# Experts' rows gathered before the layer norm's scale and bias, and memory's products ahead of the capacity test

## The chip, the core and the metric

The kernel runs on one core of a Trainium2 chip, as one program. The metric is the device time of one execution in microseconds. Of every version several executions are timed and the median is compared; one execution more is profiled. The engines are TensorE (PE; its weight loads are shown as PEld), VectorE (DVE), ScalarE (ACT), GpSimd (POOL) and SyncE (SP). Each has its own queue and works it off in order. SyncE issues nearly all loads of weights here.

## The reference

Everything is float32, on 256 tokens of 1024 channels. The first block has two layers (a mixer, a layer norm, a feed-forward part, a layer norm); in layer 1 the feed-forward part is a mixture of eight experts with two experts a token. The second block has an FFN, a second mixer that also attends to a memory of 256 tokens, and another FFN.

```python
for l in range(2):
    mix = hybrid_mixer(x, ...)
    x = layer_norm(ALPHA * x + mix, ln_mix_g[l], ln_mix_b[l])
    ff = swiglu(x, ...) if l % 2 == 0 else moe_swiglu(x, router, w1, w3, w2)
    x = layer_norm(ALPHA * x + ff, ln_ffn_g[l], ln_ffn_b[l])

def moe_swiglu(x, w_router, w1, w3, w2):
    logits = x @ w_router
    gates = softmax(top2(logits))
    # rows of x are sorted by expert; each expert e computes on its rows
    y = (silu(xb @ w1[e]) * (xb @ w3[e])) @ w2[e]
    # y times its gate is added back at the token's place

x = x + 0.5 * swiglu_ffn(rms_norm(x, ffn1_norm), ffn1_w_in, ffn1_w_out)
mem_kv = rms_norm(mem, mem_norm) @ w_mem_kv
m_k, m_v = split(mem_kv);  m_k = rms_norm(m_k per head, m_k_gain)
```

## The kernel before, in words

Products keep float32's precision by splitting: each operand is a high part (`wh`, `xTh`) and a low part (`wl`, `xTl`), and `mm3` makes three matmuls (lines 183 to 185). `part` (L172, L174) makes the parts of a weight tile of 128x1024: ScalarE copies the high part, VectorE subtracts for the low one. `load` (L166) puts SyncE's DMA of 1 MB (two such tiles) into the next of a list of buffers, `self.places`. In front of every FFN, SyncE runs ahead as far as buffers are free.

The expert stage is the function `moe`. Ahead of it, `layer_norm_T` normalises the rows (L852), transposes them (L857) and applies scale and bias by channel while it evicts the transposed tiles (L859, L860); L862 and L863 split them into `xT`. Then it applies scale and bias to the rows themselves from the tile `rows` (L867), since the experts' inputs are gathered from rows. `moe` computes the router's logits from `xT` (`lg`, L907), the two largest (L913 to L917), and each token's place in its expert (`t_pos`, L921 to L925). L930 and L931 split the rows into `xtokh` and `xtokl`.

`gather` (L980 to L1003) is a matmul of those with a one-hot matrix `oh`, 128 slots at a time, which gives the transposed inputs of one expert: `xeh` and `xel` for the four experts with most tokens ("full", 128 slots), `xef` for two pairs of the others (64 slots each). High and low rows are accumulated in two halves of a PSUM bank, which are evicted by ScalarE and VectorE (L996, L998, L1000). For each of 42 steps (expert or pair, by block of 512 hidden channels) `up` makes the products `a_up` and the gated `mos` (L1025, L1026), and `down` transposes `mos` (`t_hT`, L1032) and multiplies by the third weight (`y_y`). `combine` scales by the gate and adds the rows back by a matmul `t_comb` (L1068 to L1070) to the accumulator `acc`, which starts as x times ALPHA (L1113). Inputs of later experts are gathered between the steps.

After the last step, `memory_load` fetches memory's transposed rows (`memT`) and the weights of its keys and values (`mem_k`, `mem_v`). A test follows (L1157, L1159): `mxi` says how many rows found no place among an expert's slots; only then a loop computes them. For the data here it is skipped, but every engine loads the number and branches. After it come `layer_norm_x` (L872 on), `rms_T` (L1228 on: squares L1234, logarithm and exponential L293 and L294, scaling L1239, transposes L267, eviction L277 and L278), and `memory_keys`: 48 matmuls for the keys (`a_pA`), 48 for the values (`a_pB`), the normalisation per head (`norm_heads`, L1263 to L1267), and the copy of the values (L1346). Then the second block's first FFN starts, its first products being `a_pA<-xTh,wh` again.

The order in each queue is set by the tile framework's scheduler, which works through the program in dependence order by its own estimates; `issue_after` is a hint to it. So the order of a queue isn't that of the code. ScalarE's functions come in tables: `table` asks for a set by name (`LOGEXP` has Ln and Exp, `SILU` Silu), and the compiler adds a load (ACT_TABLE_LOAD) wherever a function isn't in the set at hand.

```python
    def part(self, raw, o=0, m=1024):
        wh = self.wp.tile([P, 1024], F32R, name="wh")
        nc.scalar.activation(wh[:, :m], raw[:, o:o + m], AF.Copy)
        wl = self.wp.tile([P, 1024], F32R, name="wl")
        nc.vector.tensor_tensor(wl[:, :m], raw[:, o:o + m], wh[:, :m].bitcast(F32), op=ALU.subtract)
```

Of the kernel before, what the change touches and what calls it, by code (L numbers as in the profile page):

```python
# [9 lines left out]
F32 = mybir.dt.float32  # L10
F32R = mybir.dt.float32r
BF16 = mybir.dt.bfloat16
I32 = mybir.dt.int32
# [15 lines left out]
NE = 8  # L29
# [74 lines left out]
class Net:  # L104
# [737 lines left out]
    def layer_norm_T(self, tp, tag, r, st, rows, name, n=4, z_="lnz", bufs=4):  # L842
# [58 lines left out]
    def moe(self, fp, x, xT):  # L901
# [23 lines left out]
        V.tensor_scalar(pos, pos, -1.0, None, op0=ALU.add)  # L925

# [50 lines left out]
        def gather(u, g):  # L977

            src = pos if u == (0,) else poss
            o = oh[u] = fp.tile([P, 2, P], F32R, name="oh", bufs=2)  # L980
            w = P // len(u)
            for t in range(2):
                for i, s in enumerate(u):
                    V.tensor_scalar(o[:, t, i * w:i * w + w], iota[:, :w], src[:, t, s:s + 1], None, op0=ALU.is_equal)
            if len(u) == 1:
                g += [fp.tile([P, 8, P], F32R, name=f"xe{c}", tag=f"xe{c}{u[0] % 2}") for c in "hl"]
            else:
                g += [fp.tile([P, 8, P], F32, name="xef")]
            for k in range(0, 8, 2):
                pg = self.ps("t", "gat").rearrange("p (a k n) -> p a k n", a=2, k=2)  # L990
                for j in range(2):
                    for a, src in enumerate((xh, xl)):
                        for t in range(2):
                            PE.matmul(pg[:, a, j, :], src[:, t, (k + j) * P:(k + j) * P + P], o[:, t],
                                      start=t + a + j == 0, stop=t == 1, skip_group_check=True)
                S.activation(g[0][:, k:k + 2, :], pg[:, 0], AF.Copy)  # L996
                if len(u) == 1:
                    self.last = V.tensor_copy(g[1][:, k:k + 2, :], pg[:, 1])  # L998
                else:
                    self.last = V.tensor_tensor(g[0][:, k:k + 2, :], g[0][:, k:k + 2, :], pg[:, 1], op=ALU.add)  # L1000
                if k == 6 and u != (0,):
                    back[u] = places(u)
                yield  # L1003
# [54 lines left out]
        def combine(py, ohT, gp):  # L1058
# [5 lines left out]
            for t in range(2):  # L1064
                for h in range(2):
                    hs = slice(h * 512, h * 512 + 512)
                    pc = self.ps("t", "comb")
                    PE.matmul(pc, ohT[:, t, :], yh[:, hs], start=True, stop=False)  # L1068
                    PE.matmul(pc, ohT[:, t, :], yl[:, hs], start=False, stop=True)
                    V.tensor_tensor(acc[:, t, hs], acc[:, t, hs], pc, op=ALU.add)  # L1070

# [40 lines left out]
        with self.tc.issue_after(self.last.ins):  # L1112
            V.tensor_scalar(acc, x, ALPHA, None, op0=ALU.mult)  # L1113
# [8 lines left out]
        for n, (u, b) in enumerate(order):  # L1122
            if n == 1:
                self.places = [(fp, f"early{i}") for i in range(EARLY)] + [(fp, "rows"), (self.ap, "xTh"), (self.ap, "xTl")] + self.places
            if n in begin:
# [15 lines left out]
        st = self.new_stats()  # L1141

        def stats():
            for t in range(2):
                for h in range(2):
                    V.bn_stats(out=st[:, t, h, :], in_=acc[:, t, h * 512:h * 512 + 512])


        cap, mxf, mxi = fp.tile([P, NE], F32, name="cap"), fp.tile([P, 1], F32, name="mxf"), fp.tile([P, 1], I32, name="mxi")
        V.tensor_scalar(cap, rank, 3.5, 64.0, op0=ALU.is_lt, op1=ALU.mult)  # L1150
        V.tensor_scalar(cap, cap, 64.0, None, op0=ALU.add)
        V.tensor_tensor(pos, pos, cap[:, None, :].to_broadcast([P, 2, NE]), op=ALU.subtract)
        V.tensor_tensor(cap, cnt, cap, op=ALU.subtract)
        V.tensor_reduce(mxf, cap, axis=AX.X, op=ALU.max)
        V.tensor_scalar(mxf, mxf, 0.0, None, op0=ALU.max)
        V.tensor_copy(mxi, mxf)
        most = nc.values_load(mxi[0:1, 0:1], min_val=0, max_val=T)  # L1157
        stats()
        with self.tc.If(most > 0):  # L1159
            ecur = fp.tile([P, 1], F32, name="ecur")  # L1160
            V.memset(ecur, 0.0)
            with self.tc.For_i(0, NE, 1) as e:
# [18 lines left out]
                for k in range(8):  # L1181
# [4 lines left out]
                    V.tensor_copy(x2[:, k, :], pg[:, :P])  # L1186
# [37 lines left out]
                stats()  # L1224
# [623 lines left out]
def build(tc, A, out):  # L1848
    with ExitStack() as ctx:
# [18 lines left out]
        with net.banks(a=2, y=4, t=2), pool("moe") as fp:  # L1868
            rows = net.load_rows(fp.tile([P, 2, D], F32, name="rows"), "ln_mix", 2, 2)
            xT = net.layer_norm_T(fp, "t", r, st, rows, "mix1", z_="mos", bufs=2)  # L1870
            r, st, mem = net.moe(fp, r, xT)
# [3 lines left out]
            net.memory_keys(fp, *mem)  # L1875
# [28 lines left out]
```

## Time and profile before

| | |
|---|---|
| median of 3 runs | 2171.85 us (2169.86 to 2173.09) |
| profiled execution's own time | 2181.34 us |
| its span in the profile | 2179.6 us |
| busy: TensorE, VectorE, ScalarE | 96%, 60%, 47% |
| mean granted clock of TensorE | 0.965 of full speed |
| DMA, mean over the span | 250 GB/s |
| the expert stage with its ends | about 605 to 1560 us of the span |

The profiled execution is 9.5 us longer than the median of the timed ones; positions in the trace belong to it. A row of the trace in order of time gives start, duration, engine, line, operation, output tile and input tiles with shapes, how many instructions were merged (x), and in brackets the engine's idle time just before with what ended it. Buffer numbers are left out of names. Suffix q (PEq, SPq) means an engine's sequencer: branches, waits, DMA issues.

### The profile page before, as it was taken

What the parts mean: (1) busy time and instruction counts of PE and PEld (TensorE: products, weight loads), DVE (VectorE), ACT (ScalarE), POOL (GpSimd) and SP (SyncE); (2) the same over time, 40 slices, a digit from 0 to 9 for tenths busy, and PEclk for the clock granted to TensorE, in tenths of its full rate; (3) what the DMA queues carried; (4) which work ended last, traced back from release to release, by engine and by line L of the source; (5) the groups of instructions that cost most, each with busy time, mean ns of one, the idle gap of its engine ahead of it and who ended that gap; (6) DMA issues with size and microseconds to landing.
All of it is one profiled execution on the core that took longest, in us unless ns stands there. A gap on an engine that the chain in (4) does not pass through costs nothing. (4 is left out here: it accounts for less than half of the span.)

```text
span 2179.6 us, 31865 instructions
## 1 busy us (share of the span) xinstructions
PE 2085.4 (96%) x12770; PEld 1606.4 (74%) x12770; DVE 1301.9 (60%) x1911; ACT 1021.4 (47%) x1453; POOL 13.0 (1%) x27
## 2 busy tenths in 40 slices
PE   8998999899979999999999999999799999999998
PEld 7887999788766565566565566554799988888997
DVE  6767954766676555555465455443655568665544
ACT  6545444464545444444354345442544444544443
POOL 0000000000000000000000000000000000000000
PEclk9979999998979999999999999999899999999999
DMA  6313675322359999999999999998455553444552
GB/s 236 103 44 117 213 261 179 136 88 98 140 181 348 363 407 381 412 419 376 404 367 396 387 404 406 417 415 352 171 188 191 187 176 125 136 164 155 184 183 97
DMA packets 78987, 545.37 MB, mean 250 GB/s; under 512 B 8960, under 2 KB 11272, under 8 KB 13936
## 3 DMA queue, kind: packets, MB, share of 16 engines
q1 hardware_dynamic: 76112, 527.40, 63.4%
q0 software_dynamic: 2720, 15.86, 2.0%
q8 instruction: 103, 1.69, 0.3%
q14 instruction: 52, 0.43, 0.1%
HBM read 536.74 MB, written 6.49 MB: 249 GB/s over the span
## 5 line engine op out<-in xcount | busy, mean ns | idle before, releaser
L174 DVE TENSOR_TENSOR wl<-raw,wh 128x1024 fp32r<-128x1024 f32 (+1 forms) x662 | 798.1, 1217 | 436.4 <-ACT wh L172 422.4
L172 ACT ACTIVATE wh<-raw 128x1024 fp32r<-128x1024 f32 (+1 forms) x662 | 690.6, 1054 | 629.0 <-PE a_pA L184 276.1
L183 PE MATMUL a_pA<-xTh,wh 128*128 128x256 f32 x1456 | 421.0, 290 | 5.9 <-ACT foxqk L620 3.3
L185 PE MATMUL a_pA<-xTh,wl 128*128 128x256 f32 x1456 | 417.9, 287 | 0.9 <-DVE wl L174 0.9
L184 PE MATMUL a_pA<-xTl,wh 128*128 128x256 f32 x1456 | 418.2, 287 | 0.0
L183 PEld LDWEIGHTS a_pA<-xTh,wh 128*128 128x128 f32 x1456 | 283.4, 195 | 13.7 <-ACT foxqk L620 5.3
L184 PEld LDWEIGHTS a_pA<-xTl,wh 128*128 128x128 f32 x1456 | 283.5, 195 | 4.8 <-issue 3.4
L185 PEld LDWEIGHTS a_pA<-xTh,wl 128*128 128x128 f32 x1456 | 283.3, 195 | 4.2 <-issue 2.7
L1021 PE MATMUL a_up<-raw,xef 128*64 128x512 f32 x896 | 213.5, 596 | 0.0
L184 PE MATMUL a_up<-wl,xeh 128*128 128x512 f32 x448 | 180.7, 403 | 0.5 <-DVE wl L174 0.4
L183 PE MATMUL a_up<-wh,xeh 128*128 128x512 f32 x448 | 177.3, 399 | 0.0
L185 PE MATMUL a_up<-wh,xel 128*128 128x512 f32 x448 | 177.1, 395 | 0.0
L1021 PEld LDWEIGHTS a_up<-raw,xef 128*64 128x64 f32 x896 | 65.2, 137 | 127.7 <-issue 122.6
L183 PE MATMUL a_pB<-wh,xTh 128*128 128x256 f32 x480 | 142.0, 297 | 5.0 <-ACT glu L620 3.1
L1026 DVE TENSOR_TENSOR mos<-mos,a_up 128x512 f32<-128x512 f32 x42 | 28.7, 684 | 192.2 <-PE a_up L1021 141.5
L184 PE MATMUL a_pB<-wl,xTh 128*128 128x256 f32 x480 | 140.4, 293 | 0.0
L185 PE MATMUL a_pB<-wh,xTl 128*128 128x256 f32 x480 | 139.4, 293 | 0.6 <-DVE xTl L278 0.6
L1054 PE MATMUL y_y<-raw,mof 128*64 128x512 f32 x448 | 132.8, 602 | 0.7 <-ACT mof L1040 0.7
L184 PEld LDWEIGHTS a_up<-wl,xeh 128*128 128x128 f32 x448 | 84.6, 189 | 35.1 <-issue 12.2
L183 PEld LDWEIGHTS a_up<-wh,xeh 128*128 128x128 f32 x448 | 84.6, 189 | 27.5 <-ACT wh L172 7.3
L185 PE MATMUL acc_acc<-wh,ffl 128*128 128x512 f32 x264 | 102.0, 392 | 0.0
L184 PE MATMUL acc_acc<-wl,ffh 128*128 128x512 f32 x264 | 101.9, 392 | 0.0
(558 smaller groups left out, 2717.9 us busy)
## 6 DMA issues: line engine op xcount, KB each, us to landing
raw<-in_moe_w_dram SPq DMA_DIRECT2D x336, 1024.0 KB, 9.3
raw<-in_ffn_in_dram SPq DMA_DIRECT2D x44, 1024.0 KB, 4.8
raw<-in_ffn_w_dram SPq DMA_DIRECT2D x33, 1024.0 KB, 4.9
raw<-in_w_in_a_dram SPq DMA_DIRECT2D x24, 1024.0 KB, 5.0
raw<-in_ffn_out_dram SPq DMA_DIRECT2D x22, 1024.0 KB, 4.8
raw<-in_w_out_dram SPq DMA_DIRECT2D x12, 1024.0 KB, 4.9
raw<-in_w_in_g_dram SPq DMA_DIRECT2D x12, 1024.0 KB, 4.9
raw<-in_w_in_b_dram SPq DMA_DIRECT2D x6, 1024.0 KB, 5.0
```

What stands on the lines that cost most here:

```text
L172: nc.scalar.activation(wh[:, :m], raw[:, o:o + m], AF.Copy)
L174: nc.vector.tensor_tensor(wl[:, :m], raw[:, o:o + m], wh[:, :m].bitcast(F32), op=ALU.subtract)
L183: mm(out, lh, rh, start=start, stop=False, skip_group_check=True)
L184: mm(out, lh, rl, start=False, stop=False, skip_group_check=True)
L185: mm(out, ll, rh, start=False, stop=stop, skip_group_check=True)
L1021: PE.matmul(ps[r], xe[0][:, k0, r], w[:, k * 512:k * 512 + 512], start=k0 == 0, stop=k0 == 7, skip_group_check=True)
L1026: V.tensor_tensor(s, s, pp[1], op=ALU.mult)
L1054: PE.matmul(py[h][r], hf[:, k, r], w[:, j * 1024 + h * 512:j * 1024 + h * 512 + 512], start=b == 0 and k == 0, stop=b == 6 and k == 3, ski ...
```

## The change

1. `layer_norm_T` gets `None` for `rows`, and the rows are left without scale and bias. They are split and gathered as they are; high and low rows add up in one PSUM region, and scale (`gain`) and bias (`shift`) are applied by channel when the gathered tile is evicted. For a full expert the result is split there.
2. The accumulator therefore starts from the normalised rows with scale, bias and ALPHA, in four instructions.
3. The count of missing places (`overflow`) is written ahead of step 4, the statistics of the last layer norm inside the last `combine`.
4. `memory_products` makes memory's 96 products and evicts both halves into `keptm` ahead of the test; `memory_keys` only normalises the keys, behind it. The buffers for `mem_k`, `mem_v` and `memT` change places.

```diff
-        with self.tc.issue_after(last.ins):
-            for t in range(2):
-                for i, op in enumerate((ALU.mult, ALU.add)):
-                    V.tensor_tensor(r[:, t, :], r[:, t, :], rows[:, i], op=op)
+        if rows is not None:
+            with self.tc.issue_after(last.ins):
+                for t in range(2):
+                    for i, op in enumerate((ALU.mult, ALU.add)):
+                        V.tensor_tensor(r[:, t, :], r[:, t, :], rows[:, i], op=op)
...
-                pg = self.ps("t", "gat").rearrange("p (a k n) -> p a k n", a=2, k=2)
+                pg = self.ps("t", "gat")[:, :T].rearrange("p (k n) -> p k n", k=2)
...
-                            PE.matmul(pg[:, a, j, :], src[:, t, (k + j) * P:(k + j) * P + P], o[:, t],
-                                      start=t + a + j == 0, stop=t == 1, skip_group_check=True)
-                S.activation(g[0][:, k:k + 2, :], pg[:, 0], AF.Copy)
+                            PE.matmul(pg[:, j, :], src[:, t, (k + j) * P:(k + j) * P + P], o[:, t],
+                                      start=t + a + j == 0, stop=a + t == 2, skip_group_check=True)
+                z = fp.tile([P, 2, P], F32, name="gz", bufs=2) if len(u) == 1 else g[0][:, k:k + 2, :]
+                for j in range(2):
+                    last = S.activation(z[:, j, :], pg[:, j, :], AF.Identity, scale=gain[:, k + j:k + j + 1], bias=shift[:, k + j:k + j + 1])
                 if len(u) == 1:
-                    self.last = V.tensor_copy(g[1][:, k:k + 2, :], pg[:, 1])
-                else:
-                    self.last = V.tensor_tensor(g[0][:, k:k + 2, :], g[0][:, k:k + 2, :], pg[:, 1], op=ALU.add)
+                    S.activation(g[0][:, k:k + 2, :], z, AF.Copy)
+                    self.last = V.tensor_tensor(g[1][:, k:k + 2, :], z, g[0][:, k:k + 2, :].bitcast(F32), op=ALU.subtract)
...
-            V.tensor_scalar(acc, x, ALPHA, None, op0=ALU.mult)
+            for t in range(2):
+                V.scalar_tensor_tensor(acc[:, t, :], x[:, t, :], ALPHA, rows[:, 0], op0=ALU.mult, op1=ALU.mult)
+                V.scalar_tensor_tensor(acc[:, t, :], rows[:, 1], ALPHA, acc[:, t, :], op0=ALU.mult, op1=ALU.add)
...
-        self.places = [(fp, "early2"), (fp, "early3")]
-        mem = self.memory_load(fp, ("early0", "early1"))
+        free = [i for i in self.places if i[1].startswith("early")]
+        self.places = free[:2]
+        mem = self.memory_load(fp, [i[1] for i in free[2:4]])
         self.places = [(self.raw, "raw")] * 4
-        combine(py[prev[0]], *back[prev[0]])
...
+        combine(py[prev[0]], *back[prev[0]], last=True)
+        mem = self.memory_products(fp, *mem)
+
+
         most = nc.values_load(mxi[0:1, 0:1], min_val=0, max_val=T)
-        stats()
         with self.tc.If(most > 0):
...
-    def memory_keys(self, fp, mT, raw, parts):
-
-        kept = self.keep_mem(fp, tag="y")
-        ps = self.proj_a(None, mT, parts=parts[:2])
+    def memory_products(self, fp, mT, raw, parts):
+
+        kept = self.keep_mem(fp, tag="xeh1")
+        self.nc.scalar.activation(self.mkT, self.proj_a(None, mT, parts=parts[:2]), AF.Copy)
+        self.nc.scalar.activation(self.mv, self.proj_b(None, mT, parts=[parts[2], self.part(raw[1], 1024)]), AF.Copy)
+        return kept
+
+    def memory_keys(self, fp, kept):
+
+        ps = self.mkT
         self.table(SILU, self.norm_heads(fp, ps, 2, self.col2("mkg"), self.mkT.rearrange("p c t -> p (c t)"), "y", "mos"))
-        ps = self.proj_b(None, mT, parts=[parts[2], self.part(raw[1], 1024)])
-        self.nc.scalar.activation(self.mv, ps, AF.Copy)
...
-            xT = net.layer_norm_T(fp, "t", r, st, rows, "mix1", z_="mos", bufs=2)
-            r, st, mem = net.moe(fp, r, xT)
+            xT = net.layer_norm_T(fp, "t", r, st, None, "mix1", z_="mos", bufs=2)
+            r, st, mem = net.moe(fp, r, xT, rows)
```

What the change moves in the queues is seen at three places. Line numbers of the changed kernel are a few higher (L930 became L934, L931 L935, L1032 L1037, L1234 L1249).

VectorE's queue at the layer norm and the router (`lnz` and `xTl` are tiles of `xT`, `lg` the logits), before:

```order
L860 TENSOR_SCALAR lnz<-t_tr,p_72 128x256 x2
L863 TENSOR_TENSOR xTl<-lnz,xTh 128x512 x2
L867 TENSOR_TENSOR x<-x,rows 128x1024 x3
L174 TENSOR_TENSOR wl<-raw,wh 128x1024
L867 TENSOR_TENSOR x<-x,rows 128x1024
L907 COPY lg<-t_pSt 128x16
L931 TENSOR_TENSOR xtokl<-x,xtokh 128x1024
L913 MAX m_6584<-lg 128x8 x2
L931 TENSOR_TENSOR xtokl<-x,xtokh 128x1024
L914 MAX_INDEX i_6587<-m_6584,lg 128x8 x2
```

and now:

```order
L935 TENSOR_TENSOR xtokl<-x,xtokh 128x1024
L860 TENSOR_SCALAR lnz<-t_tr,p_72 128x256
L935 TENSOR_TENSOR xtokl<-x,xtokh 128x1024
L860 TENSOR_SCALAR lnz<-t_tr,p_72 128x256
L863 TENSOR_TENSOR xTl<-lnz,xTh 128x512 x2
L860 TENSOR_SCALAR lnz<-t_tr,p_72 128x256 x2
L863 TENSOR_TENSOR xTl<-lnz,xTh 128x512 x2
L174 TENSOR_TENSOR wl<-raw,wh 128x1024
L909 COPY lg<-t_pSt 128x16
L915 MAX m_6580<-lg 128x8 x2
L916 MAX_INDEX i_6583<-m_6580,lg 128x8 x2
```

The four instructions with `rows` are gone, and both splits of the rows stand among the tiles of `xT` instead of behind the logits.

TensorE's queue at the thirteenth transpose of the hidden tile (`t_hT`), where the up products of a pair (`a_up<-raw,xef`) and the down products of a full expert (`y_y`) meet, before:

```order
L1021 MATMUL a_up<-raw,xef 64x512 x31
L183 MATMUL y_y_8226<-wh,moh 128x512
L183 MATMUL y_y_8227<-wh,moh 128x512
L184 MATMUL y_y_8226<-wl,moh 128x512
L185 MATMUL y_y_8226<-wh,mol 128x512
L184 MATMUL y_y_8227<-wl,moh 128x512
L185 MATMUL y_y_8227<-wh,mol 128x512
L183 MATMUL y_y_8226<-wh,moh 128x512
L183 MATMUL y_y_8227<-wh,moh 128x512
L1032 MATMUL t_hT<-call,mos 128x128 x4
```

and now:

```order
L1026 MATMUL a_up<-raw,xef 64x512 x31
L1037 MATMUL t_hT<-call,mos 128x128 x4
L183 MATMUL y_y_8260<-wh,moh 128x512
L183 MATMUL y_y_8261<-wh,moh 128x512
L184 MATMUL y_y_8260<-wl,moh 128x512
L185 MATMUL y_y_8260<-wh,mol 128x512
```

The down products that stood between the pair's last up product and the transpose now stand behind the transpose. The same is found at the nineteenth.

ScalarE's queue behind the test (`bnrs` is the layer norm's, `rmss` and `rmsx` the root mean square's, `mos` the keys' squares, `wh` the weights for the FFN, but for memory's last one in the kernel before, where it is the first `wh`), before:

```order
L873 ACTIVATE bnrs<-bnst 128x2
L309 ACT_TABLE_LOAD
L293 ACTIVATE bnrs<-bnmv,bias_1871 128x2
L294 ACTIVATE bnrs<-bnrs 128x2
L172 ACTIVATE wh<-raw 128x1024
L1234 ACTIVATE rmsx,rmss<-x 128x1024 x2
L172 ACTIVATE wh<-raw 128x1024
L1263 ACTIVATE mos<-a_pA 128x512
L293 ACTIVATE rmss<-rmss,bias_524 128x2
L294 ACTIVATE rmss<-rmss 128x2
L172 ACTIVATE wh<-raw 128x1024
L293 ACTIVATE mos<-y_nh,bias_524 128x512
```

and now, from the keys' logarithm on:

```order
L293 ACTIVATE mos<-y_nh,bias_524 128x512
L294 ACTIVATE mos<-mos 128x512
L309 ACT_TABLE_LOAD
L1249 ACTIVATE rmsx,rmss<-x 128x1024
L172 ACTIVATE wh<-raw 128x1024 x2
L1249 ACTIVATE rmsx,rmss<-x 128x1024
L172 ACTIVATE wh<-raw 128x1024
L293 ACT_TABLE_LOAD
L293 ACTIVATE rmss<-rmss,bias_524 128x2
L294 ACT_TABLE_LOAD
L294 ACTIVATE rmss<-rmss 128x2
L277 ACTIVATE xTh<-t_tr,p_2450 128x256 x8
```

The keys' normalisation and the load of Silu's table stand ahead of the squares now; three weight copies stand among the squares and ahead of the logarithm; the logarithm and the exponential have a table load each.

## Rows read from the trace of the kernel before

**Rows 1.** Busy time by stretches: span, then each engine's, clock, DMA share.

```profile
core 0: us, PE busy (x) PEld busy (x) DVE busy (x) ACT busy (x) POOL busy (x), PEclk, DMA share, GB/s
...
624.20:641.00 16.80, 11.62 (x46) 10.81 (x47) 11.66 (x54) 5.17 (x8) 0.00 (x0) 0.50 0.43 167
...
1400.00:1500.00 100.00, 98.29 (x416) 55.60 (x414) 48.64 (x44) 41.12 (x45) 0.00 (x0) 1.00 1.01 418
1530.00:1558.00 28.00, 16.67 (x113) 15.18 (x113) 21.43 (x28) 15.25 (x25) 0.54 (x1) 0.84 0.55 208
```

**Rows 2.** In order of time, VectorE, head of the expert stage.

```profile
620.04 3.49 DVE L867 TENSOR_TENSOR x<-x,rows 128x1024 f32<-128x1024 f32 x3
...
624.58 1.22 DVE L867 TENSOR_TENSOR x<-x,rows 128x1024 f32<-128x1024 f32 x1
...
625.80 1.21 DVE L931 TENSOR_TENSOR xtokl<-x,xtokh 128x1024 fp32r<-128x1024 f32 x1
...
640.80 1.23 DVE L174 TENSOR_TENSOR wl<-raw,wh 128x1024 fp32r<-128x1024 f32 x1 [2.06 <-ACT wh L172]
...
642.49 1.22 DVE L1113 TENSOR_SCALAR x<-x 128x2048 f32<-128x2048 f32 x1
```

**Rows 3.** In order of time, TensorE, the router's places and the first gather.

```profile
629.35 0.57 PE L922 MATMUL t_pos<-sel,call 128*128 128x8 f32 x2 [6.00 <-DVE g L1104]
...
631.66 0.66 PE L994 MATMUL t_gat<-oh,xtokh 128*128 128x128 f32 x2
```

**Rows 4.** Groups of instructions by line and shape, 600 to 660 us.

```profile
L998 DVE CAST xel<-t_gat 128x256 fp32r<-128x256 f32 x4 | 1.7, 422 | 2.0 <-ACT xeh L996 1.8
```

**Rows 5.** In order of time, VectorE, behind the test.

```profile
1538.09 2.48 DVE L878 SCALAR_TENSOR_TENSOR x<-x,bnmv,rows 128x1024 f32<-128x1024 f32 x2
...
1548.06 1.41 DVE L1239 TENSOR_SCALAR rmsx<-x,rmss 128x1024 f32<-128x1024 f32 x2
```

**Rows 6.** Waits from 645 to 1510 us: total, times, longest.

```profile
PEld t_hT L1032 <- DVE mos L1026: 10.8, 7, 1.7
...
PE t_hT L1032 <- DVE mos L1026: 5.3, 7, 0.9
```

**Rows 7.** One line's instructions, the test: durations in ns, first and last start.

```profile
L1159 PEldq COMPARE_BRANCH  x1: 3737/3737/3737, 1531.4 to 1531.4; - x1
```

**Rows 8.** In order of time, TensorE, the end of the stage.

```profile
1531.12 0.40 PE L1069 MATMUL t_comb<-y,ohT 128*128 128x512 f32 x1
1537.86 0.55 PE L183 MATMUL a_pA<-memT,wh 128*128 128x256 f32 x1 [6.34 <-DVEq L1159]
...
1542.24 0.28 PE L185 MATMUL a_pA<-memT,wl 128*128 128x256 f32 x1
...
1545.31 0.28 PE L185 MATMUL a_pA<-memT,wl 128*128 128x256 f32 x1
...
1559.30 0.56 PE L183 MATMUL a_pA<-xTh,wh 128*128 128x256 f32 x1
```

**Rows 9.** In order of time, ScalarE, behind the test.

```profile
1537.79 0.20 ACT L873 ACTIVATE bnrs<-bnst 128x2 f32<-128x2 f32 x1 [6.29 <-DVEq L1159]
1538.01 1.28 ACT L309 ACT_TABLE_LOAD   x1
1539.31 0.29 ACT L293 ACTIVATE bnrs<-bnmv,bias 128x2 f32<-128x2 f32 x1
1539.63 0.20 ACT L294 ACTIVATE bnrs<-bnrs 128x2 f32<-128x2 f32 x1
...
1554.78 0.83 ACT L277 ACTIVATE xTh<-t_tr,p 128x256 fp32r<-128x256 f32 x2
```

**Rows 10.** SyncE's waits from 1530 to 1560 us.

```profile
SPq L166 <- PEq L1159: 12.5, 1, 12.5
```

**Rows 11.** DMA issues of the FFN's first and second load: KB, microseconds to landing.

```profile
raw<-in_ffn_in_dram SPq DMA_DIRECT2D x1, 1024.0 KB, 5.2
...
raw<-in_ffn_in_dram SPq DMA_DIRECT2D x1, 1024.0 KB, 8.5
```

More of the change, by code (lines that the diff above doesn't have):

```diff
@@ L897, in residual_ffn1, with moe @@
         return r, st
-    def moe(self, fp, x, xT):
+    def moe(self, fp, x, xT, rows):
         nc, A, ident = self.nc, self.A, self.ident
@@ L1056, in down, with stats, combine @@
                     k += 1
-        def combine(py, ohT, gp):
+        st = self.new_stats()
+        def stats(t, h):
+            V.bn_stats(out=st[:, t, h, :], in_=acc[:, t, h * 512:h * 512 + 512])
+        def combine(py, ohT, gp, last=False):
             yh, yl = fp.tile([P, 2, D], F32R, name="y").rearrange("p a n -> a p n")
@@ L1070, in combine @@
                     V.tensor_tensor(acc[:, t, hs], acc[:, t, hs], pc, op=ALU.add)
+                    if last:
+                        stats(t, h)
         def places(u):
@@ L1112, in moe, with overflow @@
         with self.tc.issue_after(self.last.ins):
-            V.tensor_scalar(acc, x, ALPHA, None, op0=ALU.mult)
+            for t in range(2):
+                V.scalar_tensor_tensor(acc[:, t, :], x[:, t, :], ALPHA, rows[:, 0], op0=ALU.mult, op1=ALU.mult)
+                V.scalar_tensor_tensor(acc[:, t, :], rows[:, 1], ALPHA, acc[:, t, :], op0=ALU.mult, op1=ALU.add)
+        cap, mxf, mxi = fp.tile([P, NE], F32, name="cap"), fp.tile([P, 1], F32, name="mxf"), fp.tile([P, 1], I32, name="mxi")
+        def overflow():
+            V.tensor_scalar(cap, rank, 3.5, 64.0, op0=ALU.is_lt, op1=ALU.mult)
+            V.tensor_scalar(cap, cap, 64.0, None, op0=ALU.add)
+            V.tensor_tensor(pos, pos, cap[:, None, :].to_broadcast([P, 2, NE]), op=ALU.subtract)
+            V.tensor_tensor(cap, cnt, cap, op=ALU.subtract)
+            V.tensor_reduce(mxf, cap, axis=AX.X, op=ALU.max)
+            V.tensor_scalar(mxf, mxf, 0.0, None, op0=ALU.max)
+            V.tensor_copy(mxi, mxf)
         prev, py, steps = None, {}, iter(())
@@ L1124, in moe @@
                 self.places = [(fp, f"early{i}") for i in range(EARLY)] + [(fp, "rows"), (self.ap, "xTh"), (self.ap, "xTl")] + self.places
+            if n == 4:
+                overflow()
             if n in begin:
@@ L1135, in moe @@
         down(*prev, py[prev[0]])
-        self.places = [(fp, "early2"), (fp, "early3")]
-        mem = self.memory_load(fp, ("early0", "early1"))
+        free = [i for i in self.places if i[1].startswith("early")]
+        self.places = free[:2]
+        mem = self.memory_load(fp, [i[1] for i in free[2:4]])
         self.places = [(self.raw, "raw")] * 4
-        combine(py[prev[0]], *back[prev[0]])
[L1141 to L1156, printed above, removed]
+        combine(py[prev[0]], *back[prev[0]], last=True)
+        mem = self.memory_products(fp, *mem)
         most = nc.values_load(mxi[0:1, 0:1], min_val=0, max_val=T)
-        stats()
         with self.tc.If(most > 0):
@@ L1223, in moe @@
                         V.tensor_tensor(acc[:, t, hs], acc[:, t, hs], py, op=ALU.add)
-                stats()
+                for i in range(4):
+                    stats(i // 2, i % 2)
         return acc, st, mem
```

5 lines of the change are left out of this document (3 added, 2 removed).

## The prediction

> **What bounds the kernel now.** I read the busy time by stretches first, then the head of the expert stage in order of time, the waits inside the stage, the test, and the end in order of time with SyncE's waits. Times of day are positions in the profiled execution.
>
> [rows 1] The reader is to see three regimes. Late in the expert stage (1400 to 1500 us) TensorE is busy 98.29 of 100 us at full clock, though the DMA engines are busy all the time; VectorE and ScalarE are half busy. A microsecond saved on these two is worth nothing there unless TensorE waits for it. In the head (624.2 to 641.0) TensorE is busy 11.62 of 16.80 us, all of it at half the full clock (granted 0.50, the lower of its two levels), and at the end (1530 to 1558) 16.67 of 28 us at 0.84 on average. In these two a chain over VectorE and ScalarE decides, and every part of the change that can matter acts there.
>
> **Head: rows without scale and bias.** [rows 2] Before, VectorE runs four multiplications and additions by `rows` (3.49 us for three, 1.22 for one) ahead of the copy of the router's logits, and behind that copy two `xtokl` of 1.21 us. [rows 3] TensorE waits 6.00 us for the router's choice and gathers from 631.66.
> - Removed: 3.49 + 1.22 = 4.7 us of VectorE.
> - Moved: both `xtokl` (2.4 us) now stand among the tiles of `xT`, ahead of the router's product. They delay its input by up to 2.4 us and no longer stand behind the logits. I count 4.7 - 2.4 = 2.3 us earlier for the gather (ends: 0 if ScalarE's two copies `xtokh`, moved along, hold up `xT` too; 4.7 if nothing is delayed).
> - The gather has the same matmuls. Its eviction of two k tiles becomes two ScalarE instructions with scale and bias, for a full expert a copy and a VectorE subtraction besides, in place of a copy and a cast. The nearest row is the cast, 0.42 us [rows 4]; two instructions more make 0.8 us of latency for a pair of k tiles. Three of the four pairs are gathered ahead of the first expert product in the new order, so the following gathers hide most of it: I take 0.3 (0 to 0.8).
> - Added: the accumulator starts with four two-tensor instructions on 128x1024 instead of one pass of 1.22 us. The price is that of two of this form behind the test, 2.48 us [rows 5]: 4 x 1.24 = 5.0, so 3.7 us more of VectorE between the first weight splits, when TensorE uses each low half as it comes. The `wl` at 640.80 had waited 2.06 us for ScalarE [rows 2], so there is a little air: 0 to 3.7, I take 1.0.
> - They read `rows`, whose buffer is also a place for weights, so SyncE's load into it comes later, behind one other. Weights arrive ahead of their use in this stage [rows 1], and I cost this at nothing; without that cover it is a microsecond of waiting once.
>
> Head: -2.3 + 0.3 + 1.0 = **-1.0 us**, between -4.7 and +1.5.
>
> **Inside the stage: the scheduler's order.** [rows 6] TensorE's transposes of the hidden tile wait for the gated product seven times, where they directly follow the last up product of a pair: 10.8 us by the weight load (1.54 each), 5.3 by the matmul (0.76 each). The new order has two such places more, where before a full expert's down products stood between. At 1.2 us each, between the two means, **+2.4 us** (0 if the order settles otherwise on the chip, 3.1 at the upper mean). The count of missing places, written early, changes nothing: the scheduler issues these small instructions at the same early place in both kernels. The same holds for the statistics inside the last combine.
>
> **End: memory's products ahead of the test.** [rows 7, 8] Before, TensorE's last combine product starts at 1531.12 and its branch at 1531.4, which takes 3.74 us, to 1535.1; VectorE passes last, and ScalarE, which waited 6.29 us for it, goes on at 1537.79 [rows 9]. TensorE stands idle for 6.34 us and starts memory's 96 products at 1537.86, at the low clock until 1542.24. This idle time is what the move can fill. Its price is that engines run in order, so what is put ahead of the test delays what follows it:
> 1. The weight splits run on VectorE among the last additions, so I let the bulk of the products begin 1 us behind the last combine product's old place, at 1532.1. At full clock a product takes (1545.31 - 1542.24) / 27 = 0.114 us [rows 8], 96 take 10.9: they end at 1543.0. ScalarE evicts the second half (0.6 us, as one of these 128x512 tiles takes little more than half a weight copy) ahead of its own test and goes on at about 1543.6 instead of 1537.79: **5.8 us later**.
> 2. TensorE's branch moves with it. From the start of its last product to its passing it was 1535.1 - 1531.12 = 4.0 us, so it passes at about 1547.0. [rows 10] SyncE waits 12.5 us for just this before it loads the first weights of the next FFN, so these too move by 11.9 us, to about 1547.0. [rows 11] The first took 5.2 us to land, the second (issued 0.45 later) 8.5: now 1552.2 and 1555.9.
> 3. In the new order ScalarE has three weight copies, from these two loads, ahead of the logarithm for the root mean square. That waits for the second landing and a copy: 1555.9 + 1.05 = 1557.0.
> 4. The keys are normalised before that, and Silu's table is loaded behind the keys, so the logarithm and the exponential of the root mean square each load a table again, 1.28 us each [rows 9]. 1557.0 + 1.28 + 0.29 + 1.28 + 0.20 = 1560.05; VectorE's scaling, 1.41 [rows 5], 1561.5; transposes, and the first eviction of `xTh` at about 1562.1.
> 5. From the first `xTh` (1554.78 [rows 9]) to the next FFN's first product (1559.30 [rows 8]) it took 4.5 us: now 1566.6 or a little less, against 1559.30. I take **+7.0 us**.
>
> Bounds: +4 if the second load lands 3.3 us sooner, as the first did; +8.5 if Silu's own new table load (1.28 us), which I hide beside the FFN's first products, lies on the path. The exchanged places of the memory tensors cost nothing, since TensorE is still busy with the last expert's down products when the loads have landed.
>
> The Trainium skill ("ScalarE: Activation LUTs", section "What ACT_TABLE_LOAD costs") adds 1.38 us of drain to each switch of 1.283 us. By that step 4 would be 2.8 us longer and the sum 2183.1. The trace speaks against it: the load at 1538.01 is followed by the next activation at 1539.31, 1.30 us on [rows 9].
>
> **Sum.** -1.0 + 2.4 + 7.0 = +8.4 us. The profiled execution took 2181.34 us, so it would be 2189.7; the median of the three runs is 2171.85, 9.5 us below it, and on that scale the sum is **2180.3 us**, slower by 0.4%. A measurement of this kernel can tell about 0.2%, 4.3 us.
>
> **Rivals.**
> - *The head's idle time goes and the clock stays up (faster).* Place: 621 to 641 us. With neither additions nor `xtokl` between the logits and the choice, TensorE waits 1 to 3 us instead of 6.00 [rows 2, 3]; if its clock then does not fall, its 11.62 us of work at half clock take 5.8 less [rows 1], on top of -1.0: -6.8. It decides once end and inside together cost under 2.5 us: that is so if the end falls to +1.5 (the FFN's loads not tied to TensorE's branch: then squares, logarithm and scaling follow the moments directly) and the two stalls cost nothing. -6.8 + 1.5 = -5.3, **2166.5 us**. For it: the wait is there and its cause removed. Against it: the moved `xtokh` and `xtokl` make a wait ahead of the router instead, and SyncE's wait names the test. Chance 0.13.
> - *Gains and losses cancel (no change).* End +4.0, its lower bound, head -3.5, no further stall inside: +0.5, **2172.4 us**. For it: before, TensorE's own queue held the chain behind the test too, the transposes having to wait for the products. Chance 0.21.
> - *The head loses as well (slower still).* All of the accumulator's 3.7 us fall on the first splits, and the other terms reach their upper bounds: 1.5 + 3.1 + 8.5 = +13.1, **2185.0 us**. Chance 0.13.
> - *The switch of tables drains (slower still):* by the page above, 2183.1 us. Chance 0.03.
> - *The forecast,* from 2176.2 to 2184: chance 0.50.
>
> **Numbers.** Slower by over 0.2% is 0.50 + 0.13 + 0.03 = 0.66, within 0.2% 0.21, faster 0.13. The range reaches from 2168.0 (the cancelling case whole, most of the faster one left out) to 2187.0; the likeliest case's own is 2176.2 to 2184.
>
> **What would show it.** In the changed profile: the gather's first matmul some 2.3 us earlier, measured from the layer norm's statistics; the accumulator's four instructions near 640 us and TensorE waiting for `wl` close by; memory's products from about 1532 at full clock, without 6.34 us of idle ahead; then TensorE nearly idle between 1544 and 1562; SyncE's FFN loads some 11.9 us later and ScalarE waiting for their landing just ahead of the logarithm; three table loads more in all. It is wrong if the FFN's first product comes under 4 us later than before, counted from the last expert's end, or if the head gains over 3 us.

## The result, and the profile after

The changed kernel took 2188.39 us (median of 4 runs, 2184.91 to 2191.22), before beside it 2172.47: ratio 1.0072, 95% interval 1.0056 to 1.0087. The forecast was 2180.3, between 2168.0 and 2187.0. The sign was right, the time lay 1.4 us above the range, and the loss was 15.9 us where 8.4 were forecast. Run twice more, the change came out at 1.0040 (1.0018 to 1.0062) and 1.0034 (1.0016 to 1.0052) of before; the medians were 8.1 and 5.6 us apart.

The traces help more, because the part of the program that changes repeats while the rest does not. I cut it at four events: the last addition `x<-x,a_pB` in front of the layer norm (608.50 in the profile before, 607.68 after), the first gather matmul (631.66, 628.48), VectorE's last gated product `mos<-mos,a_up` (1508.33, 1512.43), and the next FFN's first product (1559.30, 1569.83). Head, stage and end are the differences:

| us | head | stage | end | sum |
|---|---|---|---|---|
| before, two profiles | 23.16, 23.16 | 876.67, 876.38 | 50.97, 51.12 | 950.8, 950.7 |
| the change, three profiles | 20.80, 20.65, 20.25 | 883.95, 884.07, 884.49 | 57.39, 57.16, 56.77 | 962.1, 961.9, 961.5 |
| difference of the means | -2.6 | +7.6 | +6.1 | +11.1 |
| forecast, cut at the same events | -2.3 | +3.7 | +7.0 | +8.4 |

So the change costs 11.1 us there. The unchanged layers ahead end anywhere between 593.8 and 608.5 us in the profiles of this study; what lies behind the FFN's first product scatters by 4 to 5 us.

The head, in order of time (engines merged), answers to [rows 2, 3]:

```profile
626.22 0.51 PE L924 MATMUL t_pos<-sel,call 128*128 128x8 f32 x2 [2.14 <-DVE g L1116]
...
628.48 0.66 PE L998 MATMUL t_gat<-oh,xtokh 128*128 128x128 f32 x2
...
639.12 2.36 DVE L1126 SCALAR_TENSOR_TENSOR x<-x,rows 128x1024 f32<-128x1024 f32 x2
...
646.53 0.50 PE L184 MATMUL a_up<-wl,xeh 128*128 128x512 f32 x1 [1.68 <-DVE wl L174]
```

TensorE waits 2.14 us for the router instead of 6.00, and the gather starts 2.4 us earlier. Then VectorE makes the accumulator's four instructions, the last of them at 644.12, and TensorE waits 1.68 us for a low half.

The waits from 645 to 1510 us answer to [rows 6]:

```profile
PEld t_hT L1037 <- DVE mos L1031: 14.3, 9, 1.7
...
PE t_hT L1037 <- DVE mos L1031: 7.0, 9, 0.9
...
PE y_y L184 <- DVE wl L174: 2.7, 2, 1.4
PE a_up L184 <- DVE wl L174: 2.6, 3, 1.7
```

and the last two before:

```profile
PE y_y L184 <- DVE wl L174: 1.4, 1, 1.4
...
PE a_up L184 <- DVE wl L174: 0.4, 1, 0.4
```

Nine stalls instead of seven, as the order had it. TensorE also waits longer for low halves of weights: 2.6 us instead of 0.4 ahead of up products (1.68 of them the wait above), 2.7 instead of 1.4 ahead of down products. The new one of these is at 1286 us; VectorE and TensorE there:

```profile
1284.94 0.69 DVE L1031 TENSOR_TENSOR mos<-mos,a_up 128x512 f32<-128x512 f32 x1 [16.13 <-PE a_up L1026]
1285.54 4.83 DVE L174 TENSOR_TENSOR wl<-raw,wh 128x1024 fp32r<-128x1024 f32 x4
...
1286.82 0.50 PE L184 MATMUL y_y<-wl,moh 128*128 128x512 f32 x1 [1.32 <-DVE wl L174]
```

VectorE has stood 16.13 us at the pair's product, which waits for the pair's last up matmul. Four weight splits are queued behind it, though ScalarE had the high halves that they start from ready by 1281.44, and TensorE waits for the first.

A part of the stage's loss is no wait. TensorE's busy time from the first gather matmul to the last gated product is 871.17 us, before 869.04, for the same 3737 matmuls. The split products themselves are longer, behind the last gather too (its last matmul starts at 1244.5 before, 1245.8 in the change). One group from 1250 to 1500 us, before and in the change (busy us, mean ns):

```profile
L183 PE MATMUL a_up<-wh,xeh 128*128 128x512 f32 x128 | 50.6, 396 | 0.0
```

```profile
L183 PE MATMUL a_up<-wh,xeh 128*128 128x512 f32 x128 | 50.9, 399 | 0.0
```

The other five groups of split products there are 1 to 3 ns longer too; the pairs' unsplit products (594 ns ahead of the gate) are not.

The test of the change (durations in ns) answers to [rows 7], and the end in order of time (engines merged) to [rows 8, 9]:

```profile
L1173 PEldq COMPARE_BRANCH  x1: 3766/3766/3766, 1546.3 to 1546.3; - x1
```

```profile
1536.85 0.28 PE L184 MATMUL a_pA<-memT,wh 128*128 128x256 f32 x1
...
1547.97 0.60 ACT L1359 ACTIVATE keptm<-a_pB 128x512 f32<-128x512 f32 x1 [4.83 <-PE a_pB L185]
1548.78 0.21 ACT L874 ACTIVATE bnrs<-bnst 128x2 f32<-128x2 f32 x1 [0.21 <-ACTq L1173]
...
1556.52 1.99 ACT L172 ACTIVATE wh<-raw 128x1024 fp32r<-128x1024 f32 x2
...
1559.45 1.04 ACT L172 ACTIVATE wh<-raw 128x1024 fp32r<-128x1024 f32 x1
1560.51 1.28 ACT L293 ACT_TABLE_LOAD   x1
...
1562.12 1.28 ACT L294 ACT_TABLE_LOAD   x1
...
1566.06 0.47 ACT L277 ACTIVATE xTh<-t_tr,p 128x256 fp32r<-128x256 f32 x1 [2.45 <-PE t_tr L267]
```

The 6.34 us of idle are gone, and the products run at full clock. But ScalarE waits 4.83 us for them ahead of its own test. From the last gated product to `bnrs` it is 36.35 us, before 29.46: 6.9 later. From `bnrs` to `xTh` it is 17.3 us, as before (17.0), in other work. The copies `wh` show no idle time ahead of them: the loads had landed 1.3 and 0.7 us earlier.

### The profile page after: what moved, and what is told of

Same layout as the page of the kernel before. It is cut to its first block, busy times and chain, and to the rows that moved or that the text cites. A ratio compares the mean times of both kernels' runs of the same rounds, so it can differ in the third digit from the quotient of the medians.

```text
span 2186.4 us, 31902 instructions
## 1 busy us (share of the span) xinstructions
PE 2082.0 (95%) x12770; PEld 1597.9 (73%) x12770; DVE 1299.5 (59%) x1902; ACT 1041.0 (48%) x1497; POOL 13.0 (1%) x27
```

## The experiments

Theory A: the end costs some 6 us because ScalarE's test stands behind the products; the stage's loss belongs to the gather part. Rivals: the test's place costs nearly all (B), or the gather does (C). "The gather part" below means all that is not part 4: parts 1 to 3 and the exchanged buffers, which no run takes apart but for the accumulator's start.

**base_again**, the kernel before, unchanged.

> The kernel before, unchanged, for a second profile. Measured against itself the ratio should be 1.000 within 0.2%. Its first profiled execution took 2181.3 us, 9 us above the median of its timed ones, so the two profiles on hand differ by 6.8 us where the medians differ by 15.9. If the profile of before was a long one by chance, this one should be near 2172, and its stretch from the layer norm's statistics to the next FFN's first product should be shorter than the 950.8 us of the first profile, by up to 4 or 5 us. If the first profile's stretch is typical (950.8 within 1 us), the missing 4 to 5 us lie outside of the stage.

Measured 1.0001 (0.9982 to 1.0021); the stretch 950.7 us, so it is typical, and the program's first two layers scatter.

**e1_products_back** undoes part 4 but for the exchanged buffers.

```diff
-        mem = self.memory_products(fp, *mem)
...
-    def memory_products(self, fp, mT, raw, parts):
...
-    def memory_keys(self, fp, kept):
...
-        ps = self.mkT
+    def memory_keys(self, fp, mT, raw, parts):
...
+        kept = self.keep_mem(fp, tag="y")
+        ps = self.proj_a(None, mT, parts=parts[:2])
```

> Memory's products and the values' eviction again behind the test, all else as changed. Theory A (the end's chain grew by some 6 us, the rest comes from the gather with its longer evictions and from the accumulator's start): the end loses its cost, and +4 to +6 us over before remain, about 2177. Theory B (nearly the whole loss is the test's place, through the branch and the late loads): within 2 us of before, about 2172, since the head gained 2.4 us. Theory C (the gather is the cost): 2183 or more.

Measured 1.0029 (1.0008 to 1.0050), 2181.55. Head 20.66, stage 884.05, end 49.61. The end's loss is gone, the stage's stays. The stretch is 3.6 us longer than before, the time some 6, at the upper edge of A. `bnrs` comes 27.48 us behind the last gated product, 2.0 earlier than before; this kernel has the statistics in the last combine.

**e2_products_only** does part 4 alone in the kernel before.

```diff
         combine(py[prev[0]], *back[prev[0]])
+        mem = self.memory_products(fp, *mem)
...
-            net.memory_keys(fp, *mem)
+            net.memory_keys(fp, mem)
```

> The kernel before with only memory's products and their evictions put ahead of the test. Theory A: +6 to +7 us, about 2179. Theory B: +14 us or more, about 2187. Theory C: within 3 us of before.

Measured 1.0028 (1.0007 to 1.0048), 2181.37: by time A. Head and stage are those of before (23.18, 876.77), the end 62.11, worse than in the change; by the traces that is 11.3 us, between A and B. Here a copy did wait for a landing, between the squares, and the table loads follow from 1552.09:

```profile
1545.57 1.06 ACT L172 ACTIVATE wh<-raw 128x1024 fp32r<-128x1024 f32 x1 [1.70 <-DMA raw<-in_ffn_in_dram]
```

**e3_one_table** writes the keys ahead of the root mean square and asks for Silu's table behind both.

```diff
-        self.table(SILU, self.norm_heads(fp, ps, 2, self.col2("mkg"), self.mkT.rearrange("p c t -> p (c t)"), "y", "mos"))
+        self.norm_heads(fp, ps, 2, self.col2("mkg"), self.mkT.rearrange("p c t -> p (c t)"), "y", "mos")
...
-            xT = net.rms_T("t", fp, x, net.col2("f1n"), tag="xtokh")
             net.memory_keys(fp, mem)
+            xT = net.rms_T("t", fp, x, net.col2("f1n"), silu=True, tag="xtokh")
```

> The change with the keys' normalisation written ahead of the root mean square and Silu's table asked for behind both, so that the two new loads ahead of the logarithm and the exponential are gone and the load of Silu's table in the FFN too. If the loads lie on the path as the prediction's step 4 has it: 2.6 us less than the change, about 2185.8; with another 1.3 us if the load ahead of the keys' end also leaves the path, 2184.5. If ScalarE has slack there (the chain hangs on the weights' landing instead): within 1 us of the change, 2188.

Measured 1.0037 (1.0019 to 1.0056). The end is 54.47 us, 2.3 to 2.9 less than in the change's three profiles. The two loads are gone, and Silu's stands behind the exponential instead of ahead of the squares: the loads lay on the path. The two alone are 2.56 us; what Silu's adds isn't told apart.

**after_again**, the change itself.

> The change itself again. Profiles of the stage repeat (before twice: 950.8 and 950.7 us from the layer norm's first statistics to the next FFN's first product; the change 962.2), so theory A has a true difference of 11.4 us: about ratio 1.0052. The first runs showed 15.9 us (1.0056 to 1.0087). If these runs again show 15 or more while the same stretch is 962 us, something outside of this stretch is slower in the changed kernel; if they show 9 to 13, the first 15.9 was 11.4 and the scatter of single runs.

Measured 1.0040 (1.0018 to 1.0062), the stretch 961.9. The first 15.9 us don't come back.

**e4_raw_free**: the skipped loop's weights go to other buffers.

```diff
-                            w = self.raw.tile([P, 2048], F32, name="raw")
+                            w = fp.tile([P, 2048], F32, name="raw", tag=f"early{c}")
```

> The change, with the weights of the loop behind the test (which is skipped) placed in other free buffers, so that SyncE's loads for the next FFN no longer wait for TensorE's branch. If step 3 of the prediction is right (the logarithm waits for the second landing): 2 to 3 us less than the change. If the loads only just arrive in time, as the changed profile shows (the weight copies at 1556.5 and 1559.5 us have no idle time ahead of them): 0 to 1 us less, unless the scheduler puts the copies elsewhere, and then by the ScalarE time of up to three copies, 3 us.

A miss: 1.0073 (1.0049 to 1.0097), end 63.45. The FFN's loads went out from 1497.07 on, and memory's own stand behind them: issued at 1503.93 and 1504.36, they took 18.3 and 20.3 us to land (5.0 and 7.2 in the change). In the new order memory's splits stand behind the last additions, and TensorE waits for their low halves:

```profile
1533.53 0.58 PE L184 MATMUL a_pB<-wl,memT 128*128 128x256 f32 x1 [5.81 <-DVE wl L174]
```

That is 29.5 us behind the last gated product, in the change 22.7, and after the wait the clock is at half (granted 0.50 from 1529.1 to 1539.4; in the change it is full until 1551.3). So the values are evicted 7.9 us later, counted the same way; ScalarE's next weight copy waits 11.56 us for TensorE meanwhile. It tells nothing on step 3 of the prediction. What tells is that behind the test, with these copies gone, `bnrs` to `xTh` took 14.6 us instead of the 16.7 to 17.3 of the change's profiles: the copies' own time on ScalarE counts there.

**e5_acc_plain** and **v1_split_evict** are e1_products_back with one edit more each: the accumulator's start by the one pass of before, which leaves out scale and bias of the rows in the accumulator, and half of a gather's eviction on VectorE.

```diff
-            for t in range(2):
-                V.scalar_tensor_tensor(acc[:, t, :], x[:, t, :], ALPHA, rows[:, 0], op0=ALU.mult, op1=ALU.mult)
-                V.scalar_tensor_tensor(acc[:, t, :], rows[:, 1], ALPHA, acc[:, t, :], op0=ALU.mult, op1=ALU.add)
+            V.tensor_scalar(acc, x, ALPHA, None, op0=ALU.mult)
```

```diff
-                for j in range(2):
-                    last = S.activation(z[:, j, :], pg[:, j, :], AF.Identity, scale=gain[:, k + j:k + j + 1], bias=shift[:, k + j:k + j + 1])
+                S.activation(z[:, 0, :], pg[:, 0, :], AF.Identity, scale=gain[:, k:k + 1], bias=shift[:, k:k + 1])
+                self.last = V.tensor_scalar(z[:, 1, :], pg[:, 1, :], gain[:, k + 1:k + 2], shift[:, k + 1:k + 2], op0=ALU.mult, op1=ALU.add)
```

> As e1_products_back, but the accumulator starts with the one pass of before; it leaves out scale and bias of the rows in the accumulator. Theory S1 (the accumulator's four instructions starve the first weight splits): from the first gather matmul to the last pair's gated product it takes 2 to 3 us less than the 884.0 of e1_products_back. Theory S2 (the longer evictions of the gather, and the transposes moved by the order, hold the stage up): at most 1 us less; the order of this kernel has two of the stalled transposes fewer, which alone gives 1.9 us.

> As e1_products_back, but of each gathered pair of k tiles ScalarE takes one and VectorE the other, as the layer norm does. The order has ten stalled transposes where e1_products_back has thirteen and before eleven. S2: 3 us less in the stage by the stalls (0.95 each), and up to 1 us more by shorter evictions ahead of weight copies: 880 us from the first gather matmul to the last gated product, and about 2 us above before in all. S1: no change, since VectorE's load at the first splits is larger.

Measured 1.0007 (0.9982 to 1.0033) and 1.0011 (0.9992 to 1.0031); stage 883.09 and 884.92. By positions (the last up matmul of each pair of experts, counted from the first gather matmul) the accumulator is worth 2.15 us: the first pair's last up matmul comes 73.27 us behind the first gather matmul in e5_acc_plain, 75.43 in e1_products_back. But 1.2 of these are lost again later, in another order. v1_split_evict has fewer stalled transposes by its order than e1_products_back (10 against 13; 7 waits against 9 in the traces) and no shorter stage: their count doesn't foretell the time.

**w1_held, w3_held_late, w0_before_held** hold a full expert's last down products behind the pair's up products, and the pair's transpose behind those; the first two in e1_products_back, the third in the kernel before. w3_held_late also writes the accumulator's four instructions three steps later.

```diff
+                        with (self.tc.issue_after(self.lastup.ins) if held and k == 3 else contextlib.nullcontext()):
...
+            with (self.tc.issue_after(self.lasty.ins) if len(u) == 2 else contextlib.nullcontext()):
```

> As e1_products_back, with the last four of a full expert's down products held behind the pair's up products and the pair's transposes behind those, so that Silu and the product run beside them. The order has 4 transposes directly behind a pair's up product where e1_products_back has 13. Theory S2 (the order's stalls of about 1.4 us each are the main loss in the stage): 7 to 12 us less than the 884.0 us from the first gather matmul to the last pair's gated product, so below the 876.5 of before, and 3 to 8 us faster than before in all. Theory S3 (held products come late and something else stalls, the split weights or the DMA): no less than 882 us.

> As w1_held, and the accumulator's four instructions are issued three steps later, when the first experts' weights have been split. S1 (they cost 2 us at the first weight splits, the stall of 1.7 us on a low half included): 1.5 to 2 us less than w1_held from the first gather matmul to the last gated product. If the later release of the buffer of rows, a place for weights, costs as much: no gain.

> The kernel before with the held products and nothing else. If the stall is worth 1.35 us apiece (what the change's two new ones cost by position), its seven waits are worth up to 9 us: 867 to 872 us instead of 876.5, and the gain in time 5 to 9 us. With the 0.76 of the matmuls' own idle time: 3 to 5 us.

None was shorter: 1.0053 (1.0031 to 1.0074), 1.0051 (1.0035 to 1.0068) and 0.9993 (0.9977 to 1.0009); stage 883.82, 883.91 and 877.58. Of w1_held S3 came true (no less than 882). w3_held_late doesn't test what it was for: the scheduler put two of the four instructions at 611.57 and two at 614.75, ahead of the last low halves for the router, and the head is 25.67 us, 5.0 longer than in e1_products_back. Why the stage is no shorter is seen in the waits of w0_before_held from 645 to 1510 us (its lines stand one lower; the kernel before has one such wait, of 1.4 us):

```profile
PE y_y L185 <- DVE wl L175: 10.6, 8, 1.4
```

The transposes no longer wait, and the held products do instead, for low halves that VectorE makes only behind the pair's product. TensorE's idle time only moved; that VectorE's wait at the product is behind both is argued from the order of its queue and not tested by itself.

**e8_evict_behind**: the products ahead of the test, their evictions behind it; the skipped loop uses the `y` banks of PSUM.

```diff
-        self.nc.scalar.activation(self.mkT, self.proj_a(None, mT, parts=parts[:2]), AF.Copy)
-        self.nc.scalar.activation(self.mv, self.proj_b(None, mT, parts=[parts[2], self.part(raw[1], 1024)]), AF.Copy)
-        return kept
+        ps = self.proj_a(None, mT, parts=parts[:2])
+        return ps, self.proj_b(None, mT, parts=[parts[2], self.part(raw[1], 1024)])
...
+        self.nc.scalar.activation(self.mv, pv, AF.Copy)
```

> The change with memory's products ahead of the test, but their evictions behind it; the skipped loop uses other PSUM banks. ScalarE then passes the test without waiting for the products. Theory E1 (the end's loss comes from ScalarE's wait for the second half ahead of its test): from the last pair's gated product to the next FFN's first product 51 us or less instead of 57.4, as before. Theory E2 (TensorE's branch behind the products, and with it the keys' small product and the FFN's loads, hold the rest up): 54 to 57 us.

Measured 0.9988 (0.9968 to 1.0008); end 46.80, E1. ScalarE and TensorE in order of time:

```profile
1525.98 0.20 ACT L874 ACTIVATE bnrs<-bnst 128x2 f32<-128x2 f32 x1 [6.14 <-DVEq L1173]
...
1528.32 0.35 PE L184 MATMUL a_pA<-memT,wh 128*128 128x256 f32 x1 [2.06 <-PEq L1173]
...
1533.60 1.06 ACT L172 ACTIVATE wh<-raw 128x1024 fp32r<-128x1024 f32 x1 [2.40 <-DMA raw<-in_ffn_in_dram]
```

ScalarE passes with VectorE's statistics, 27.48 us behind the last gated product instead of 36.35, which is where it passes in e1_products_back without the products. Since nothing ahead of the test needs the products' end, the scheduler let TensorE take its branch in the middle of them, and it idles 2.06 us for it. The root mean square's logarithm is ahead of the keys' again, without table loads.

**e10_end_only, e9_evict_behind_raw_free, e15_end_and_half_rows**: this end in the kernel before; e8 with the edit of e4; e10 with half of the rows' scale and bias issued behind the router's choice.

> The kernel before with memory's products ahead of the test and their evictions behind it, and no other part of the change. If the gather part alone makes the stage's loss: the stage as before (876.5 us from the first gather matmul to the last pair's gated product), the end about 46.8 us as in e8_evict_behind, in all 4 us faster than before, about 0.998. If the end's gain needs the exchanged places or the statistics in the combine: end 49 to 51 us, no difference in time.

> As e8_evict_behind, with the skipped loop's weights in other buffers, so that the next FFN's loads don't wait for TensorE's branch. ScalarE waited 2.4 us for such a load in e8_evict_behind: if that is all that changes, the end is 2 us shorter, 45 us. But the order puts all products ahead of the test again and gives back the table loads ahead of the logarithm: if these decide, the end is 50 us or more and the loads were never the matter.

> As e10_end_only, and of the rows' scale and bias the second half is done behind the router's choice. The first gather matmul should come 1 to 2 us earlier after the layer norm's statistics (21 to 22 us instead of 23.2). The order has 13 stalled transposes where before has 11: if the stage's time goes by these stalls, it loses 2.7 us there and the sum is 1 us slower than e10_end_only; if by the gather's longer evictions and the accumulator, which are as before here, it keeps the gain.

e10: 0.9998 (0.9979 to 1.0017); stage 876.52, so the stage's loss belongs to the gather part, and the end 50.16, 3.4 us longer than in e8_evict_behind. 2.0 of these lie ahead of `bnrs` (29.45 us behind the last gated product, as before), 1.9 behind the first `xTh`, where the keys' exponential and the load of Silu's table stand among the evictions. Which of the parts that it lacks brings e8's order isn't shown. e9: 1.0082 (1.0062 to 1.0102), end 62.54, for e4's reason: memory's loads land 18.3 and 20.8 us after their issue, TensorE waits 5.82 us for a low half, and three copies that wait for TensorE stand ahead of ScalarE's test. e15: 1.0008 (0.9992 to 1.0024); head 21.55, stage 877.44, end 54.60, with a wait of 4.01 us for an FFN load ahead of the squares. In its stage stand the same new stalls as in the change (265, 392 and 653 us behind the first gather matmul, there 269, 397 and 658), and yet it loses only 0.9 us against before. Its split products are as long as before's (396 ns in the group shown above).

**after_third**, the change a third time.

> The change a third time. If the true effect is what the profiles show from the layer norm on (8.0 us) and the first 15.9 was scatter of the stretch ahead of it: ratio 1.0037, between 1.002 and 1.0055. If the changed program is slower by 15.9 us and the profiles were lucky: 1.006 or more. From the layer norm's statistics to the end of the program the profile should again show 1578.7 us within 0.5.

Measured 1.0034 (1.0016 to 1.0052). To the end of the program the profile showed 1581.7 us, 3 more than the 1578.7 expected: the FFNs and the second mixer scatter too.

No version was clearly faster than before; e8_evict_behind came nearest by time (stretch 951.5 us), e10_end_only by the traces (949.9, before 950.7).

## Why the prediction was right or wrong

The sign, the head and the size of the end were right; **the stage was mis-sized**, +7.6 us where the terms gave 0.3 + 1.0 + 2.4 = 3.7. Its sum priced two stalled transposes and took every other matmul of the stage as before.

- *Head, -2.3:* measured -2.6, by the mechanism named. Of the rival with the clock a little came true: the wait shrank to 2.14 us, and the half clock lasted 7.8 us behind the first gather matmul (to 636.3) instead of 9.4 (631.66 to 641.1). At the first pair's up matmuls e5_acc_plain stands 0.7 us ahead of before, on top of the head.
- *The accumulator, 1.0:* 2.15 measured. The bounds held (0 to 3.7); the air ahead of the one `wl` that I took as cover wasn't there for the next. In the prediction's head sum the upper bound of +1.5 doesn't follow from its terms: 0 + 0.8 + 3.7 is 4.5, and the slowest rival's 13.1 would be 16.1.
- *Inside the stage, +2.4: the step that failed.* I counted two stalls at a price. Both came, at 897 and 1025 us, and a third place with a late low half, at 1287; by the positions of the pairs' up matmuls the change falls back by 5.9 us between the first pair step and the last. A count of stalled transposes does not give the time: with 4 (w1_held), 10 (v1_split_evict) and 13 (e1_products_back) of them by the order the stage took 883.8 to 884.9. e10 and e2 show that the loss belongs to the gather part.
- *What the stage cost instead.* e15, with before's gather and stalls in the same three places, tells the terms apart. The order's stalls: in e15 TensorE is idle for 3.0 us more than before (10.7 us in the stage against 7.6), but its matmuls are busy for 2.3 us less, and the stage is 0.8 us longer than in the first profile of before. The accumulator: the change has 2.1 us of idle time on top of e15's, 1.68 of them in one wait for a low half. The products: the change has 4.4 us more of busy time than e15 (871.17 against 866.76) for the same matmuls. Most of that is a term that the sum lacks. Worked out from the starts of the rows, from one split product to the next it takes 237.7 to 238.4 ns on average in the six profiles without the gather part and 240.1 to 240.9 in the twelve with it; with some 1880 of them, 2 ns are about 4 us. Evictions beside the products can't be all of it, since those behind the last gather are longer too. Why a product of the same shape takes 2 ns more stays open.
- *End, +7.0:* +6.1. Step 1 was right (5.8 forecast, 6.9 measured), and e8 shows its cause: with the evictions moved behind the test, ScalarE passes 8.9 us earlier. Step 2's branch took 3.77 us as assumed. Step 3, the wait for the loads, was wrong for the change: issued from 1550.16, they landed 5.1 and 8.2 us later, at 1555.2 and 1558.8, and ScalarE copied at 1556.52 and 1559.45 without having waited, so its own instructions set the time; in e2 and e8 there was such a wait, of 1.70 and 2.40 us. Step 4, two table loads (2.56 us), is borne out by e3: 2.3 to 2.9 us with Silu's load moved as well. By the Trainium skill ("ScalarE: Activation LUTs", section "What ACT_TABLE_LOAD costs") two switches would be an estimated 5.3 us; the measurement decides, and the rows of the two loads show 1.28 us each.
- *The measured 15.9* lies above the 11.1 that the traces give; the two later comparisons, 8.1 and 5.6 by the medians, lie below it. The prediction's 8.4, like 11.1 (1.0051), is inside the two later intervals and below the first. Where the first runs lost the rest isn't settled; the layers ahead of the change scatter enough for it.

## What to carry to other kernels

Work put ahead of a branch to fill one engine's idle time also puts its evictions ahead of the other engines' branch; put the matmuls ahead and leave in PSUM what others must fetch. A wait in an in-order queue can't be argued away at the engine that shows it: find the instruction that holds the queue (here, as it seems, VectorE's product for the pair, with four weight splits behind it). Moving those splits was not tried. Where a scheduler sets the order, price an edit by what it does to whole queues over the stage. Compare the length of an engine's own instructions with their waits: 2 ns on each of 1880 products were more than both stalls together. And time the unchanged kernel more than once.

## What the runs showed that was not expected

TensorE's branch over the skipped loop took 3.74 and 3.37 us in the two profiles of before, 3.77 to 3.87 in the change's, and 3.35 to 3.87 over all; the other engines' took 0.05 to 0.07. Freed loads can cost: e4 and e9 issued the FFN's first loads at 1497.07 and 1503.89, before the last expert's end and ahead of memory's, and came out at 1.0073 and 1.0082 of before, since memory's weights then came late. And the same program's first two layers ended up to 14.7 us apart between profiles, which is more than the change itself.
